# Attention in a two-layer trunk: row sums from a column of ones, the mask added on TensorE, head pairs on the two halves of the array

## The chip, the cores and the metric

The kernel runs on one core of one Trainium2 chip. The metric is the device time of one execution in microseconds (us); where several runs are given, it is their median. The engines are called by the profile's names: PE is the matrix engine (TensorE) and PEld its weight loads, DVE the vector engine, ACT the scalar engine, POOL the GpSimd engine, SP the queue that starts most transfers. PSUM is the small memory that PE writes to and that DVE and ACT read.

## The reference

Two layers. Each has a feed-forward block, a token mixer, a second feed-forward block and a norm. The mixer projects the normed rows (512 tokens, width 1024) once and splits the result into three groups of heads whose outputs are joined and projected back:

```python
y_conv = conv_module(u_conv, ...)                 # gated, causal depthwise conv of width 31, LayerNorm, swish: 384 channels
y_swa  = sliding_window_attention(q, k, v, sinks) # 6 query heads over 2 key/value heads of width 64
y_mem  = memory_attention(qm, mk, mv)             # 4 heads of width 64 over 256 memory tokens
h = h + concat([y_conv, y_swa, y_mem]) @ w_out
```

Both attentions are softmax attentions over at most 256 keys. In the sliding window each block of 128 queries sees its own block of keys and the one before, cut by a band:

```python
scores = einsum(q, keys of this block and the one before) * 64 ** -0.5
scores = where(0 <= rel < 128, scores, -inf)
probs = softmax(concat([scores, sink]))[..., :-1]   # the sink enters the sum, and has no value
out = einsum(probs, v)
```

All of it is fp32. The kernel holds its large projections as a high and a low part in a 32-bit format that PE multiplies in one pass (fp32r) and makes three products of them; the small attention products are plain fp32.

## The kernel before

A layer's feed-forward blocks are long runs of fp32r matmuls, and they are not changed, but for the memory's keys and values, which are made in the middle of the first block. The change is in the mixer. It is written as a list of steps (`ORDER`, line 45): three input projections of the convolution (`c`), queries and keys (`q`), values (`v`), four steps `r0` to `r3` for the memory attention and four steps `w0` to `w3` for the window, one for each block of 128 tokens, then the convolution's taps (`t`) and its norm and swish (`s`). That list is not the order on the chip. A scheduler of the language reorders the instructions of the whole program by its own estimate of times, and each engine then runs its instructions strictly in the resulting order: an instruction that waits holds up all behind it on its engine.

The steps of the attention, with the names that the text uses:

- **Scores.** For a pair of heads (a *pair* is the two heads that share 128 columns, one on partitions 0 to 63 and one on 64 to 127) one fp32 matmul multiplies the 128 rows of queries with a key tile of twice the width, in which each head's other half is zero (`kz` for the window, `mz` for the memory): lines 716 and 733. PSUM tiles `mm` take the result. The scores are negated, so that the row's maximum is a minimum.
- **Minimum.** In a window one DVE instruction per head (line 719) adds the band's mask, writes the masked scores back and gives the row's minimum, which starts from the sink. In the memory steps one reduction per pair does (line 734).
- **Exponential.** ACT (line 685), one instruction per head, which also sums its row into `den` by `accum_out`; that appears in the trace as a further ACT instruction that reads the accumulator.
- **Weighted sum** (`weighted`). PE transposes the 128x128 blocks of probabilities into a `pt` tile (line 690), ACT copies it to `aux` (line 692), PE multiplies it with the values into `po` (line 695).
- **Normalise and transpose** (`attended`). For a window DVE adds the sink's part to `den` (line 724) and inverts it (725); DVE multiplies `po` with the inverse (line 701), PE transposes the result into a `cf` tile (line 704), ACT and DVE split it into the high and the low part (lines 135 and 136).
- **Taps.** The depthwise convolution is 93 DVE instructions in a layer, 3 of line 741 and 90 of line 744, each on 128x512 elements. They depend on nothing in the attention. Their sum over channels goes through PE at line 753 to the norm and swish (lines 753 to 763).
- **Output projection.** PE first multiplies the attention's five tiles (120 matmuls for 8 output tiles), then the convolution's three (72 matmuls), all of 512 columns in fp32r.

## Time and profile before

| | us |
|---|---|
| median of 3 runs | 1847.12 |
| lowest and highest run | 1841.6, 1849.46 |
| the profiled execution's own time | 1840.85 |
| its span | 1839.1 |
| PE busy in the span | 1777.9 (97%) |
| DVE, ACT, POOL busy | 1297.8, 895.5, 188.3 |

The profiled execution is one of its own, 6.3 us below the median of the three. Its span leaves out 1.75 us around the program. In the rows of a timeline the first number is the start and the second the duration of one instruction, or of a few alike that follow each other; a duration of PE is longer than the step to the next start, since matmuls are pipelined, so times of PE are best taken from start to start. A plain fp32 matmul shows as two records, one for each of its two passes, and a transpose as one. The attention of layer 0 lies between 468 and 526 us and that of layer 1 between 1371 and 1429 us.

### The profile page before, as it was taken

The numbers are of one execution on the slowest core, as the hardware profiler recorded it, in microseconds if no ns is written. First come the engines' busy times: TensorE is split into PE (matmuls) and PEld (weight loads), VectorE is DVE, ScalarE is ACT, GpSimd is POOL, SyncE is SP. The second block draws the span as 40 slices with busy tenths as digits, with TensorE's granted clock in tenths as the row PEclk, the third lists the DMA queues.
The fourth block names the chain that finished last, engine by engine and source line by source line (L and its number), as shares of the span: only waits on it lengthen the run. The fifth ranks groups of instructions, "written<-read, shape, count | busy, mean of one in ns | idle before, by whom it ended". The sixth has DMA issues, their size and how long they took to land.

```text
span 1839.1 us, 28085 instructions
## 1 busy us (share of the span) xinstructions
PE 1777.9 (97%) x10892; PEld 1581.9 (86%) x10892; DVE 1297.8 (71%) x1978; ACT 895.5 (49%) x1459; POOL 188.3 (10%) x194
## 2 busy tenths in 40 slices
PE   6999999998899999999999999999989999999997
PEld 5989999877677989898888898988776889898986
DVE  7967666579956866666678586666789577675755
ACT  5556444354656535453565463535456455353532
POOL 4001000005101000000010010000240010000000
PEclk8999999999999999999999999999999999999998
DMA  9565645263038556565465565643530576474622
GB/s 278 125 172 159 177 130 155 63 159 101 15 77 200 118 141 167 143 169 141 133 154 139 160 170 141 170 118 92 117 105 1 144 162 158 134 181 122 171 78 75
DMA packets 92437, 248.87 MB, mean 135 GB/s; under 512 B 9488, under 2 KB 11792, under 8 KB 92304
## 3 DMA queue, kind: packets, MB, share of 16 engines
q1 hardware_dynamic: 76752, 190.45, 34.0%
q0 software_dynamic: 15552, 56.63, 17.3%
q8 instruction: 85, 1.39, 0.3%
q14 instruction: 48, 0.39, 0.1%
HBM read 244.95 MB, written 2.10 MB: 134 GB/s over the span
## 4 chain that ended last, share of the span: by engine, by line
PE 76%; DVE 10%; issue 7%; DMA 4%; ACT 2%; POOL 1%; SPq 0%; POOLq 0%; DVEq 0%; ACTq 0%
PE mm L162 11%; PE mm L163 10%; PE mm L161 10%; PE po L163 8%; PE po L161 8%; PE po L162 8%; PE pt L161 5%; PE pt L162 5%; PE pt L163 5%; DVE there L744 3%; DVE wlo L136 1%; DMA wlo<-in_w1a 1%; DVE xlo L146 1%; DMA wlo<-in_wconv 1%; DVE st L229 1%
## 5 line engine op out<-in xcount | busy, mean ns | idle before, releaser
L135 ACT ACTIVATE whi<-raw 128x1024 fp32r<-128x1024 f32 (+4 forms) x372 | 342.3, 924 | 513.3 <-PE mm L162 263.9
L136 DVE TENSOR_TENSOR wlo<-raw,whi 128x1024 fp32r<-128x1024 f32 (+4 forms) x372 | 392.0, 1056 | 123.8 <-ACT whi L135 122.5
L162 PE MATMUL mm<-glo,whi 128*128 128x512 f32 x752 | 293.9, 391 | 1.0 <-DVE glo L136 1.0
L161 PE MATMUL mm<-ghi,whi 128*128 128x512 f32 x752 | 289.8, 391 | 5.2 <-ACT ghi L379 4.5
L163 PE MATMUL mm<-ghi,wlo 128*128 128x512 f32 x752 | 292.8, 389 | 0.0
L163 PE MATMUL po<-mh,wlo 128*128 128x256 f32 x864 | 244.6, 283 | 1.4 <-DVE wlo L136 1.4
L161 PE MATMUL po<-mh,whi 128*128 128x256 f32 x864 | 244.8, 283 | 0.0
L162 PE MATMUL po<-ml,whi 128*128 128x256 f32 x864 | 244.6, 283 | 0.0
L161 PE MATMUL pt<-xhi,whi 128*128 128x256 f32 x864 | 243.4, 283 | 1.0 <-DVE g L347 0.7
L163 PE MATMUL pt<-xhi,wlo 128*128 128x256 f32 x864 | 243.9, 283 | 0.0
L162 PE MATMUL pt<-xlo,whi 128*128 128x256 f32 x864 | 243.8, 283 | 0.0
L443 DVE SCALAR_TENSOR_TENSOR h<-mm,h 128x512 f32<-128x512 f32 x128 | 87.7, 688 | 134.5 <-PE mm L163 134.5
L161 PEld LDWEIGHTS mm<-ghi,whi 128*128 128x128 f32 x752 | 140.9, 188 | 35.9 <-ACT ghi L379 6.2
L161 PEld LDWEIGHTS pt<-xhi,whi 128*128 128x128 f32 x864 | 165.1, 192 | 3.0 <-DVE g L347 1.1
L163 PEld LDWEIGHTS po<-mh,wlo 128*128 128x128 f32 x864 | 165.8, 192 | 1.6 <-DVE wlo L136 1.6
L162 PEld LDWEIGHTS mm<-glo,whi 128*128 128x128 f32 x752 | 141.4, 188 | 30.0 <-DVE glo L136 1.9
L162 PEld LDWEIGHTS pt<-xlo,whi 128*128 128x128 f32 x864 | 165.7, 192 | 1.1
L161 PEld LDWEIGHTS po<-mh,whi 128*128 128x128 f32 x864 | 165.8, 192 | 0.9 <-ACT part L366 0.2
L163 PEld LDWEIGHTS mm<-ghi,wlo 128*128 128x128 f32 x752 | 141.2, 188 | 29.2
L162 PEld LDWEIGHTS po<-ml,whi 128*128 128x128 f32 x864 | 165.8, 192 | 0.6
L163 PEld LDWEIGHTS pt<-xhi,wlo 128*128 128x128 f32 x864 | 165.5, 192 | 0.0
L744 DVE SCALAR_TENSOR_TENSOR there<-ypad,par,there 128x512 f32<-128x512 f32 x180 | 133.7, 759 | 0.7
(272 smaller groups left out, 3306.4 us busy)
## 6 DMA issues: line engine op xcount, KB each, us to landing
raw<-in_w2a SPq DMA_DIRECT2D x48, 384.0 KB, 3.7
raw<-in_w2b SPq DMA_DIRECT2D x48, 384.0 KB, 4.0
raw<-in_w1a SPq DMA_DIRECT2D x26, 512.0 KB, 3.7
raw<-in_w3a SPq DMA_DIRECT2D x26, 512.0 KB, 4.3
raw<-in_w1b SPq DMA_DIRECT2D x26, 512.0 KB, 3.8
raw<-in_w3b SPq DMA_DIRECT2D x26, 512.0 KB, 3.7
wsum<-in_w1a SPq DMA_DIRECT2D x18, 512.0 KB, 4.5
wsum<-in_w3a SPq DMA_DIRECT2D x18, 512.0 KB, 4.5
```

Source lines behind the costliest of these rows:

```text
L135: A.activation(hi, x, AF.Copy)
L136: on.tensor_tensor(out=lo, in0=x, in1=hi.bitcast(F32), op=ALU.subtract)
L146: V.scalar_tensor_tensor(out=lo, in0=x, scalar=col, in1=hi.bitcast(F32), op0=ALU.mult, op1=ALU.subtract)
L161: T.matmul(ps, a[0], b[0], start=first, stop=False, **more)
L162: T.matmul(ps, a[0], b[1], start=False, stop=False, **more)
L163: tail[0] = T.matmul(ps, a[1], b[0], start=False, stop=last, **more)
L229: V.tensor_tensor(out=self.sums[0], in0=self.sums[0], in1=sq, op=ALU.add)
L443: V.scalar_tensor_tensor(out=h[:, d, :], in0=ps, scalar=0.5, in1=h[:, d, :], op0=ALU.mult, op1=ALU.add)
L744: V.scalar_tensor_tensor(out=cv[:, c, :], in0=ypad[:, c, j : j + S], scalar=conv_w[:, c, j : j + 1], in1=cv[:, c, :], op0=ALU.mult, op1=AL ...
```

## The change

- **Key tiles without zeros.** `kT` and `mT` hold both heads, one on each half of the partitions. `scored` makes two matmuls per pair, each on 64 rows of the array: head 0 on rows 0 to 63 and head 1 on rows 64 to 127, of 256 columns each (128 in `w0`) where there was one of 512 (256 in `w0`). Head 0 of every pair goes to one PSUM tile and head 1 to another.
- **The mask on PE.** In a window each of these tiles is first written by an fp32r matmul of the identity with the mask (line 686), and the scores are added to it in PSUM.
- **Two pairs per minimum.** A window handles its pairs as (0, 1) and (2). One reduction takes the minimum of the same head of two pairs (line 736), and a small instruction then takes the sinks in (line 737). The memory steps take both pairs at once (line 752).
- **Sums from a column of ones.** The values get a 65th column of ones, so the weighted sum gives the sum of the row in column 64 of `po`. ACT's `accum_out` goes, and a window's `den` becomes `po`'s column 64 plus the sink's part (line 742), a memory step's inverse comes straight from it (line 755).
- **Fewer, wider splits.** Two neighbouring tiles of `y` are split at once, and the transposes of `attended` use a `pt` tile instead of `cf`. The copies that spread keys over two zero-padded tiles become one copy, and the zero fills become fills of the ones.

```diff
+        def scored(cs, W, q, k, masked):
+            pp = [mm().rearrange("p (c k) -> p c k", c=2)[:, 0 : len(cs), 0:W] for _ in range(2)]
+            if masked:
+                for ps in pp:
+                    T.matmul(ps, identr, maskr[:, 256 - W : 256].unsqueeze(1).to_broadcast([P, len(cs), W]), start=True, stop=False,
+                             skip_group_check=True)
+            for n, c in enumerate(cs):
+                for i in range(2):
+                    e = blk(i, HD)
+                    T.matmul(pp[i][:, n, :], q(c)[e], k(c)[e], start=not masked, stop=True, skip_group_check=True)
+            return pp
...
-                A.activation(pr[:, i, 0 : nk * P], scores[:, i, 0 : nk * P], AF.Exp, bias=nm[:, n : n + 1], scale=-1.0,
-                             accum_out=den[:, n : n + 1])
+                A.activation(pr[:, i, 0 : nk * P], scores[i], AF.Exp, bias=nm[:, n : n + 1], scale=-1.0)
...
-            V.tensor_tensor(out=heads(z), in0=po, in1=rd.unsqueeze(2).to_broadcast([P, n, HD]), op=ALU.mult)
-            pt = bank([P, c1 - c0, P], "cf")
+            V.tensor_tensor(out=heads(z), in0=po[:, :, 0:HD], in1=rd.unsqueeze(2).to_broadcast([P, n, HD]), op=ALU.mult)
+            pt = bank([P, c1 - c0, P], "pt")
...
-            po = bank([P, NH, HD], "po")
-            for c in range(CC):
-                ps = bank([P, 2, 256], "mm")
-                T.matmul(ps[:, :, 0:W], qT[:, c, blk(b)], kz[:, :, b0 * P : b0 * P + W], start=True, stop=True)
+            po = bank([P, NH, HD + 1], "po")
+            nmv, sinks = (x.rearrange("p (c i) -> p i c", i=2) for x in (nm, nsink[:, l, :]))
+            for cs in ((0, 1), (2,)):
+                pp = scored(cs, W, lambda c: qT[:, c, blk(b)], lambda c: kT[:, b0 * P : b0 * P + W], True)
+                z = slice(cs[0], cs[-1] + 1)
                 for i in range(2):
-                    n = 2 * c + i
-                    V.tensor_tensor_reduce(out=ps[:, i, 0:W], in0=ps[:, i, 0:W], in1=mask[:, 256 - W : 256], scale=1.0,
-                                           scalar=nsink[:, l, n : n + 1], op0=ALU.add, op1=ALU.min, accum_out=nm[:, n : n + 1])
-                weighted(c, nk, ps, nm, den, lambda j, i: vn[:, b0 + j, blk(i, HD)], po)
+                    V.tensor_reduce(out=nmv[:, i, z], in_=pp[i], axis=AX.X, op=ALU.min)
+                V.tensor_tensor(out=nmv[:, :, z], in0=nmv[:, :, z], in1=sinks[:, :, z], op=ALU.min)
+                for n, c in enumerate(cs):
+                    weighted(c, nk, [ps[:, n, :] for ps in pp], nm, lambda j, i: vn[:, b0 + j, i, :], po)
             V.tensor_tensor(out=es, in0=sink, in1=nm, op=ALU.add)
             A.activation(es, es, AF.Exp)
-            V.tensor_tensor(out=den, in0=den, in1=es, op=ALU.add)
-            V.reciprocal(rd, den)
+            V.tensor_tensor(out=rd, in0=po[:, :, HD], in1=es, op=ALU.add)
+            V.reciprocal(rd, rd)
             attended(b, 0, CC, po, rd)
```

The scheduler puts the new instructions in another order, and moves old ones too. Three places show it. The numbers behind the names tell buffers apart.

**Place 1: DVE in layer 0, ahead of the minima of window step `w1`.** Line 744 before and line 763 now are taps; a row that ends in x11 is eleven of them. Before (the tiles `mm_4533` and `mm_4549` hold the scores of `w1`):

```order
L722 TENSOR_TENSOR a1_4473<-rw_98,a0_4472 128x6
L744 SCALAR_TENSOR_TENSOR there_3738<-ypad_106,par_96,there_3738 128x512
L136 TENSOR_TENSOR glo_3755<-cf_4422,ghi_3754 128x128
L744 SCALAR_TENSOR_TENSOR there_3738<-ypad_106,par_96,there_3738 128x512
L724 TENSOR_TENSOR a2_4474<-a2_4474,a1_4473 128x6
L744 SCALAR_TENSOR_TENSOR there_3738<-ypad_106,par_96,there_3738 128x512
L136 TENSOR_TENSOR glo_3755<-cf_4422,ghi_3754 128x128
L725 RECIPROCAL a3_4475<-a2_4474 128x6
L719 ISA mm_4533,a0_4528<-mm_4533,cst_94,nsink_110 128x256
```

and now, where the tiles `mm_4529` and `cf_4530` hold the scores of the first two pairs of `w1`:

```order
L740 TENSOR_TENSOR a1_4465<-rw_98,a0_4464 128x6
L763 SCALAR_TENSOR_TENSOR there_3737<-ypad_106,par_96,there_3737 128x512 x2
L136 TENSOR_TENSOR glo_3753<-pt_4459,ghi_3752 128x2x128
L763 SCALAR_TENSOR_TENSOR there_3737<-ypad_106,par_96,there_3737 128x512 x11
L742 TENSOR_TENSOR a2_4466<-po_4467,a1_4465 128x6
L736 TENSOR_REDUCE a0_4525<-mm_4529 128x2
L736 TENSOR_REDUCE a0_4525<-cf_4530 128x2
L736 TENSOR_REDUCE a0_4525<-mm_4564 128x1
L736 TENSOR_REDUCE a0_4525<-mm_4565 128x1
```

From the first minimum of `r0` on, both orders hold the same 37 taps of layer 0 (36 in layer 1). Before, 13 of them (12 in layer 1) stand ahead of the first minimum of `w1`, and the others are spread up to the end of `r3`. Now 34 (32 in layer 1) stand ahead of it, and none behind the minima of `w2`.

**Place 2: PE in layer 0, from the first transposes of `w1` to the scores of `w2`.** Before:

```order
L690 MATMUL pt_4539<-cst_94,uu_3744 128x128 x4
L716 MATMUL mm_4601<-here_3737 128x512
L690 MATMUL pt_4555<-cst_94,pr_3747 128x128 x2
L704 MATMUL cf_4518<-cst_94,aux1_3742 128x128 x3
L716 MATMUL mm_4617<-here_3737 128x512
L716 MATMUL mm_4633<-here_3737 128x512
L695 MATMUL po_4532<-here_3737,aux0_3741 128x64 x4
```

and now, where `mm_4602` and `mm_4637` belong to head 0 of the pairs and `cf_4603` and `mm_4638` to head 1:

```order
L703 MATMUL pt_4542<-cst_94,uu_3742 128x128 x4
L686 MATMUL mm_4602<-maskr_117 128x512
L691 MATMUL mm_4602<-here_3736 128x256 x2
L686 MATMUL cf_4603<-maskr_117 128x512
L691 MATMUL cf_4603<-here_3736 128x256 x2
L686 MATMUL mm_4637<-maskr_117 128x256
L691 MATMUL mm_4637<-here_3736 128x256
L686 MATMUL mm_4638<-maskr_117 128x256
L691 MATMUL mm_4638<-here_3736 128x256
L708 MATMUL po_4528<-here_3736,aux0_3739 128x65 x4
```

In every window the products of one half of the array stand together, and a mask product on all 128 rows stands between the two halves. Only in the memory steps do the halves stand side by side, in 3 of the 8 steps alternating and in 5 as two of one half and then two of the other. Over a layer PE changes 39 times between products on 128 and on 64 rows.

**Place 3: DVE and PE in layer 0, from the end of `w1` to `w2`.** DVE now:

```order
L742 TENSOR_TENSOR a2_4527<-po_4528,a1_4526 128x6
L736 TENSOR_REDUCE a0_4598<-mm_4602 128x2
L736 TENSOR_REDUCE a0_4598<-cf_4603 128x2
L736 TENSOR_REDUCE a0_4598<-mm_4637 128x1
L743 RECIPROCAL a2_4527<-a2_4527 128x6
L736 TENSOR_REDUCE a0_4598<-mm_4638 128x1
L737 TENSOR_TENSOR a0_4598<-a0_4598,nsink_110 128x2x2
L714 TENSOR_TENSOR aux1_3740<-po_4528,a2_4527 128x384
```

and PE now:

```order
L708 MATMUL po_4528<-here_3736,aux0_3739 128x65 x8
L717 MATMUL pt_4590<-cst_94,aux1_3740 128x128 x3
L703 MATMUL pt_4615<-cst_94,uu_3742 128x128 x4
L691 MATMUL mm_4674<-mT_114,there_3737 128x256 x2
L691 MATMUL cf_4675<-mT_114,there_3737 128x256 x2
```

The first DVE row reads column 64 of `po_4528`, which the first PE row completes; before, the sum at its place (line 724) read nothing that PE makes. The minima of `w2` stand behind it on DVE, the multiplication of `w1` (line 714) behind those, and on PE the transposes of that product (line 717) stand straight behind the weighted sum.

66 lines of the change are left out of this document (35 added, 31 removed).

## The prediction

> **What bounds the kernel now.** I read the page first, then the stages of the two mixers by windows, then the timeline of DVE and PE in them.
>
> ```profile
> span 1839.1 us, 28085 instructions
> PE 1777.9 (97%) x10892; PEld 1581.9 (86%) x10892; DVE 1297.8 (71%) x1978; ACT 895.5 (49%) x1459; POOL 188.3 (10%) x194
> PE 76%; DVE 10%; issue 7%; DMA 4%; ACT 2%; POOL 1%; SPq 0%; POOLq 0%; DVEq 0%; ACTq 0%
> ```
>
> PE sets the time nearly everywhere; what the change is worth is decided where PE waits, in the attention.
>
> ```profile
> core 0: us, PE busy (x) PEld busy (x) DVE busy (x) ACT busy (x) POOL busy (x), PEclk, DMA share, GB/s
> 468.50:486.90 18.40, 16.43 (x92) 11.22 (x93) 18.34 (x49) 12.60 (x43) 3.29 (x3) 1.00 0.06 19
> 486.90:490.50 3.60, 0.71 (x7) 0.48 (x6) 3.60 (x16) 0.95 (x4) 0.95 (x1) 0.83 0.00 0
> 490.50:495.00 4.50, 4.50 (x14) 3.10 (x15) 4.43 (x12) 3.31 (x15) 0.00 (x0) 0.50 0.01 2
> 495.00:520.00 25.00, 24.75 (x164) 18.95 (x163) 23.69 (x67) 17.71 (x62) 0.00 (x0) 0.98 0.00 1
> 526.00:554.40 28.40, 28.40 (x139) 23.86 (x138) 9.51 (x17) 10.42 (x17) 2.52 (x4) 1.00 0.51 128
> ```
>
> In layer 0 DVE is full from 468.5 to 495 (26.4 of 26.5 us), for most of it with taps. It feeds PE too late once, at 486.9 to 490.5, and PE then runs at a granted clock of 0.50 for 4.5 us. From there on PE is full, and its output projection hides the swish, whose work on DVE and ACT is light. So the time of a mixer is when `w1`'s first transposes start on PE, plus what PE has left from there to the next stage.
>
> ```profile
> 490.45 1.14 PE L690 MATMUL pt<-cst,uu 128*128 128x128 f32 x4 [2.88 <-ACT uu L685]
> 491.38 1.91 PE L716 MATMUL mm<-here 128*128 128x512 f32 x2
> 503.94 1.02 PE L716 MATMUL mm<-here 128*128 128x512 f32 x2
> 504.80 0.49 PE L704 MATMUL cf<-cst,aux 128*128 128x128 f32 x3
> 505.13 1.90 PE L695 MATMUL po<-here,aux 128*128 128x64 f32 x16
> 506.86 0.61 PE L690 MATMUL pt<-cst,uu 128*128 128x128 f32 x4
> 507.31 1.02 PE L716 MATMUL mm<-here 128*128 128x512 f32 x2
> 570.75 0.39 PE L161 MATMUL mm<-xhi,whi 128*128 128x512 f32 x1
> 570.98 0.39 PE L162 MATMUL mm<-xlo,whi 128*128 128x512 f32 x1
> 1394.78 0.89 PE L690 MATMUL pt<-cst,uu 128*128 128x128 f32 x4 [2.05 <-ACT uu L685]
> 1473.75 0.39 PE L161 MATMUL mm<-xhi,whi 128*128 128x512 f32 x1
> ```
>
> The rows of 570.75 and 1473.75 begin the next stage, so that rest takes 80.3 us in layer 0 and 79.0 us in layer 1 now. From start to start: a score product of 512 columns takes 0.86 us (both passes), a weighted sum 2 x 1.73/16 = 0.216, a transpose 0.45/4 = 0.11, an fp32r product of 512 columns 0.227 (0.23 in the row).
>
> **What the change moves ahead of `w1`.** DVE costs, from start to start:
>
> ```profile
> 471.20 0.68 DVE L734 TENSOR_REDUCE m<-mm 128x2 f32<-128x512 f32 x1
> 471.80 0.41 DVE L514 TENSOR_REDUCE hs<-hsq 128x4 f32<-128x256 f32 x1
> 472.13 0.68 DVE L734 TENSOR_REDUCE m<-mm 128x2 f32<-128x512 f32 x1
> 472.73 0.41 DVE L519 TENSOR_TENSOR gg<-gg,rsq 128x256 f32<-128x256 f32 x1
> 473.06 0.74 DVE L744 SCALAR_TENSOR_TENSOR there<-ypad,par,there 128x512 f32<-128x512 f32 x1
> 473.72 0.54 DVE L741 TENSOR_SCALAR there<-ypad,par 128x512 f32<-128x512 f32 x1
> 474.18 0.16 DVE L515 TENSOR_SCALAR hv<-hs 128x4 f32<-128x4 f32 x1
> 486.94 0.45 DVE L719 CUSTOM_DVE_ANT_0 mm<-mm,cst,nsink 128x256 f32<-128x256 f32 x1
> 487.31 0.14 DVE L719 DVE_READ_ACCUMULATOR2_ANT a<- 128x1 f32 x1
> 507.96 0.55 DVE L701 TENSOR_TENSOR aux<-po,a 128x384 f32<-128x384 f32 x1
> 508.43 0.28 DVE L136 TENSOR_TENSOR glo<-cf,ghi 128x128 fp32r<-128x128 f32 x1
> 508.62 0.48 DVE L719 CUSTOM_DVE_ANT_0 mm<-mm,cst,nsink 128x256 f32<-128x256 f32 x1
> 1374.14 0.68 DVE L734 TENSOR_REDUCE m<-mm 128x2 f32<-128x512 f32 x1
> ```
>
> A tap takes 0.66, a reduction of 512 elements 0.60 and of 256 0.33, other work on 256 elements 0.33, line 701 0.47, a split of 128 elements 0.19, small ones 0.09. The taps never wait, so DVE runs its order without a gap, as it does now. Counted from the first minimum of `r0` (471.20 and 1374.14, unmoved, since the same 56 or 57 taps stand ahead of it), the new order holds, up to the multiplication of `w0` that PE's transposes of line 717 wait for ahead of `w1`: 36 taps (23.8), one line 760 (0.5), minima of `r0` and `r1` (2.4), of `w0` (about 1.1) and of `w1` (1.9), three line 714 (1.1), two splits (0.7), two scalings of queries (0.7) and a dozen small ones (1.1), 33.1 us in all. In layer 1 there are 34 taps and one scaling and a 0.6 us multiplication, 31.9. With 0.4 us for three transposes and the handover, `w1`'s first transposes start at 504.7 and 1406.4 instead of 490.45 and 1394.78: **+14.3 and +11.6 us**. DVE's work itself is less, not more: a window takes 2 x 0.60 + 2 x 0.33 + 0.2 = 2.1 where six times 0.40 were, and five splits become three, some 3 us a layer; but the gain lies behind `w1`, where DVE no longer sets the time.
>
> **What PE has left from there.** 65 transposes (7.2), 52 weighted sums (11.2; the 65th column costs nothing, since 64 columns in 0.108 a pass are far above what 512 in 0.43 make of them), 20 score products of 256 columns, each at half of 0.86 (8.6), masks of `w2` and `w3` (2 x (2 x 0.227 + 2 x 0.113) = 1.4), line 772 (0.9), 192 products of the output projection (43.5) and the swish's sums and broadcast (1.7 and 0.8, in the chain of waits): 75.2 us.
> ```profile
> 533.46 1.68 PE cf L186 x16
> 540.52 0.89 PE pt L199 x8
> ```
>
> The same count of the old work gives 73.8, so 6.5 and 5.2 us of the old 80.3 and 79.0 are waits and the slow clock. To the 75.2 I add what the new order makes of waits.
>
> *The sums from the ones.* Line 742 reads what the last weighted sum writes, the next step's minima wait behind it on DVE, the product for line 717 behind these, and PE has line 717 straight after the weighted sum. So PE stands still for line 742, the minima but the last, 743 and 714, and the handovers:
>
> ```profile
> 521.30 0.42 DVE L701 TENSOR_TENSOR aux<-po,m 128x256 f32<-128x256 f32 x1 [0.24 <-PE po L695]
> 489.83 0.47 ACT L685 ACTIVATE uu<-mm,a 128x256 f32<-128x256 f32 x1 [1.95 <-DVE a L719]
> ```
>
> DVE waited 0.24 us there for PE, ACT in the second row for DVE; I take 0.35 for both handovers of a wait. Between `w1` and `w2` that is 2.6 + 0.35, between `w2` and `r2` 1.85 + 0.35 less 0.55 of scores that fill it, between `r2` and `w3` 1.95 + 0.35, between `w3` and `r3` 1.85 + 0.35: 9.1 us. Exponentials and copies that nothing on PE covers (`r2`'s copies, `w3`'s last minimum and first exponentials at 0.47 each) add about 2. **11 us a layer.** ACT no longer reads accumulators, which shortens these a little and nothing else, since ACT is at 71% of its time there (17.71 of 25 us).
>
> *Array halves and changes of mode.* No two halves run side by side in a window: a mask product on all rows stands between. In `r2` and `r3` at best one product of 0.43 in a pair is hidden, 0.9 a layer at most; I take none. What a change between 128 and 64 rows costs, no row shows. Below nothing is excluded by the count above; the upper end is a pipeline that empties at each, which is what a product's duration exceeds its spacing by:
>
> ```profile
> L163 PE MATMUL mm<-ghi,wlo 128*128 128x512 f32 x752 | 292.8, 389 | 0.0
> L161 PEld LDWEIGHTS mm<-ghi,whi 128*128 128x128 f32 x752 | 140.9, 188 | 35.9 <-ACT ghi L379 6.2
> ```
>
> 0.389 less 0.227 is 0.16, and with a weight load laid bare 0.35. Of the 39 changes of a layer 20 come after `w1`'s first transposes: 0 to 7 us; I take half of 0.16 each, 1.6, as loads are mostly pulled ahead. [...]
>
> *The clock.* By the costs above PE has some 17 us of work in the 33 us ahead of `w1` (`r0`, `r1`, `w0`, the scores of `w1`), and eleven taps in a row (7.3 us) leave it a gap just before. After 3.6 us with little work it ran at 0.50 for 4.5 us; the same again costs 2.2.
>
> **The sum.** 75.2 + 11 + 1.6 + 2.2 = 90.0 for 80.3 and 79.0: +9.7 and +11.0. With +14.3 and +11.6 that is +46.6, from 1840.85 of the profiled execution to 1887. That execution lies 6.3 under the median, whose sum would be 1894. I say **1889**. What I cost at nothing: the mask's copy and the fills at the start lie under the first weight transfers, and would cost their length, under 1 us, without that cover; the fewer key copies on ACT lie under PE's projections.
>
> **The rivals.** *The delay alone*: PE finds other work in every wait, and the clock holds. The rest is then 75.2, and the sum +14.3 + 11.6 - 5.1 - 3.8 = +17, 1864. For it speaks that PE hardly waits after 495 now; against it that the order leaves nothing between the weighted sum and line 717.
>
> *Faster: the halves overlap.* Were head 0 and head 1 of each pair side by side, nine pairs of windows would save 0.43, three of `w0` 0.22 and eight of the memory 0.43, 8 us a layer, less 2.4 of masks: -11 in all, 1836, from the point at which PE and not DVE sets `w1`'s start. [...] The order keeps the halves apart in windows and the taps ahead of `w1`, so I give it little; that the change does not do what its title says about halves is the likelier reading.
>
> *No change*: DVE free of taps from `w2` on serves PE so fast that waits vanish, and the old slow clock goes too. That needs 8.5 us a layer less than the delay alone, more than all the waits there are now (6.5 and 5.2): 1841 to 1847 at the very best.
>
> *Changes of mode dear*: 0.35 each and the slow clock after every wait, 5 us: 75.2 + 11 + 7 + 7 = 100, sum +67, 1911; with longer handovers 1920.
>
> **How the numbers follow.** Forecast with its own spread 0.80; delay alone 0.09; dear changes 0.06; no change 0.03; overlap 0.02. A difference of under 0.5% (9 us) cannot be told from none here. So slower 0.95, same 0.03, faster 0.02. The range: below, the delay with half of the waits and no mode cost, 1840.85 + 17 + 11 = 1869, lowered a little for the delay alone, 1865; above, dear changes, 1915.
>
> **What would show it.** In the changed profile `w1`'s first transposes start near 504.7 and 1406.4, with a PE wait for DVE ahead of them and a clock near 0.5 after; PE waits at line 717, put down to line 714, some 2 us four times a layer; the next stage begins near 595 in layer 0; behind `w2` DVE is no longer full; starts of line 691 lie 0.43 apart. I am wrong if `w1` starts as early as now, if line 717 waits for nothing, or if the rest takes under 80 us.

## The result and the profile after

| | before | after |
|---|---|---|
| median, us | 1844.62 | 1947.58 |
| lowest and highest run | 1841.6, 1849.46 | 1946.65, 1951.77 |
| ratio (95% interval) | | 1.056 [1.0536, 1.0583] |
| profiled execution's span | 1839.1 | 1944.9 |
| mean granted clock | 0.988 | 0.946 |

The change makes the kernel 103 us slower; forecast were 42 to 47. The direction was right, the forecast size was less than half of the measured one, and the time lies above the range of 1865 to 1915. The page of the changed kernel (span; busy time, share and instructions of each engine):

```profile
span 1944.9 us, 28120 instructions
PE 1853.8 (95%) x11004; PEld 1641.7 (84%) x11004; DVE 1298.5 (67%) x1914; ACT 881.9 (45%) x1352; POOL 186.5 (10%) x191
```

PE is busy 76 us longer, but hardly with more work. The next two fences show the windows view, for each layer from the first score product of the memory to `w1`'s first transposes, and from there to the next stage's first product. First the changed kernel:

```profile
core 0: us, PE busy (x) PEld busy (x) DVE busy (x) ACT busy (x) POOL busy (x), PEclk, DMA share, GB/s
468.31:510.86 42.55, 30.39 (x127) 22.13 (x128) 38.44 (x75) 13.71 (x35) 4.55 (x3) 0.63 0.03 8
510.86:620.71 109.85, 98.89 (x436) 79.32 (x436) 39.02 (x81) 42.20 (x84) 5.00 (x5) 0.77 0.25 64
1423.69:1464.43 40.74, 30.10 (x127) 22.17 (x126) 37.38 (x71) 14.04 (x36) 2.27 (x2) 0.64 0.03 8
1464.43:1578.82 114.39, 103.39 (x436) 81.52 (x436) 39.64 (x82) 41.61 (x83) 5.00 (x5) 0.74 0.25 61
```

and the kernel before, in the same columns:

```profile
468.49:490.45 21.96, 17.11 (x97) 11.65 (x97) 21.90 (x63) 13.51 (x47) 4.24 (x3) 0.97 0.05 16
490.45:570.75 80.30, 79.04 (x411) 62.83 (x411) 55.55 (x126) 46.23 (x120) 4.99 (x5) 0.96 0.35 88
1371.75:1394.78 23.03, 17.81 (x97) 12.22 (x95) 21.09 (x58) 14.10 (x48) 2.28 (x2) 0.93 0.05 15
1394.78:1473.75 78.97, 76.58 (x410) 61.29 (x411) 55.49 (x127) 46.62 (x120) 4.99 (x5) 1.00 0.36 90
```

The columns give the length of the stretch, the busy time of each engine, and the granted clock (PEclk). Three quantities come out of each row: PE's idle time (length less busy), its work at full clock (busy times clock) and the loss to the clock (busy times one less the clock). PEclk is a mean over the whole length, idle time included, and has two digits, so the last two are good to some 3 us in a long stretch. In layer 0 and layer 1 together the work grows by 5 us (from 185.6 to 191.1), the idle time by 31 (from 13.7 to 44.7), and the loss to the clock by 67 (from 5.0 to 71.7). These three make the 103 us. Counted only where PE is busy, with the pieces of full and of half clock that the traces record, the work grows by 7 and the loss by 65: the reading stays.

In the timeline of PE in the changed kernel (start, duration, line, with the wait ahead and what ended it in brackets) stand the places that the prediction spoke of:

```profile
468.31 0.48 PE L691 MATMUL mm<-mT,there 64*128 64x256 f32 x1 [0.65 <-ACT there L551]
468.32 0.48 PE L691 MATMUL cf<-mT,there 64*128 64x256 f32 x1
...
510.20 0.88 PE L717 MATMUL pt<-cst,aux 128*128 128x128 f32 x3 [4.28 <-DVE a L740]
510.86 1.06 PE L703 MATMUL pt<-cst,uu 128*128 128x128 f32 x4
511.58 0.78 PE L686 MATMUL mm<-maskr 128*128 128x512 f32 x1
514.28 0.79 PE L686 MATMUL cf<-maskr 128*128 128x512 f32 x1
...
530.38 0.87 PE L717 MATMUL pt<-cst,aux 128*128 128x128 f32 x3 [2.81 <-DVE a L737]
...
554.48 0.69 PE L717 MATMUL pt<-cst,aux 128*128 128x128 f32 x2 [2.11 <-DVE aux L714]
...
567.66 0.87 PE L717 MATMUL pt<-cst,aux 128*128 128x128 f32 x3 [2.30 <-DVE aux L714]
...
1464.43 1.06 PE L703 MATMUL pt<-cst,uu 128*128 128x128 f32 x4
```

`w1`'s first transposes start at 510.86 and 1464.43. The waits at line 717 are there, 2 to 4 us each. The memory's products on the two halves run side by side (468.31 and 468.32). A window's do not, and at half clock a mask and two products take 2.7 us (511.58 to 514.28). The windows view shows the point that decides:

```profile
479.13:533.75 54.62, 42.57 (x138) 30.62 (x138) 31.91 (x69) 14.18 (x40) 2.99 (x2) 0.50 0.00 1
533.75:543.99 10.24, 8.20 (x48) 5.93 (x47) 2.01 (x5) 2.65 (x6) 0.00 (x0) 1.00 0.00 0
543.99:571.30 27.31, 21.93 (x88) 18.29 (x89) 6.58 (x19) 8.93 (x22) 0.00 (x0) 0.50 0.00 1
1465.00:1475.00 10.00, 10.00 (x24) 5.71 (x23) 0.76 (x3) 0.88 (x3) 1.27 (x1) 0.50 0.00 0
```

From 1465 to 1475 PE never waits, and its clock is 0.50 all the time. The first three rows are the pieces of half and full clock in layer 0. In all traces here the clock in an attention goes between 1.00 and 0.50 in pieces of 3.41 us or whole multiples of it: these three are 16, 3 and 8 such lengths, and the slow ones in the two attentions of the kernel before are 2 and 1.

### The profile page after: what moved, and what is told of

It reads as the page before. It is cut to its first block, busy times and chain, and to the rows that moved or that the text cites. A ratio compares the mean times of both kernels' runs of the same rounds, so it can differ in the third digit from the quotient of the medians.

```text
span 1944.9 us, 28120 instructions
## 1 busy us (share of the span) xinstructions
PE 1853.8 (95%) x11004; PEld 1641.7 (84%) x11004; DVE 1298.5 (67%) x1914; ACT 881.9 (45%) x1352; POOL 186.5 (10%) x191
## 4 chain that ended last, share of the span: by engine, by line
PE 79%; DVE 10%; issue 6%; DMA 2%; ACT 1%; POOL 1%; SPq 0%; DVEq 0%; POOLq 0%; ACTq 0%
PE mm L161 10%; PE mm L162 10%; PE mm L163 10%; PE po L163 8%; PE po L161 8%; PE po L162 8%; PE pt L162 5%; PE pt L161 5%; PE pt L163 5%; DVE there L763 3%; PE po L708 2%; PE mm L691 2%; PE pt L703 1%; DVE wlo L136 1%; DMA wlo<-in_w1a 1%
```

## Experiments

Line numbers in an experiment's rows are its own. The kernels with "u" undo parts of the change in the changed kernel; those with "a" make one part alone in the kernel before. The table reads the stretch from the memory's first score product to the next stage in layer 0 in the way shown above, with the same error. Each ratio is to runs of the kernel before that were made together with it, whose medians lie between 1842.4 and 1846.7, so times of kernels made at different times compare to some 4 us. The scheduler makes a new order for each kernel, and each price includes that.

| kernel | us | ratio to before (95%) | stretch, us | idle | loss to clock | work at full clock |
|---|---|---|---|---|---|---|
| before | 1844.6 | | 102.3 | 6.1 | 2.9 | 93.3 |
| after | 1947.6 | 1.056 [1.0536, 1.0583] | 152.4 | 23.1 | 34.9 | 94.4 |
| u_rows | 1913.3 | 1.0371 [1.0351, 1.0391] | 138.4 | 26.6 | 19.0 | 92.8 |
| u_ones | 1930.9 | 1.0466 [1.0422, 1.051] | 151.2 | 9.4 | 42.6 | 99.3 |
| u_mask | 1933.8 | 1.0485 [1.0468, 1.0501] | 151.9 | 20.8 | 39.3 | 91.8 |
| u_pair | 1980.9 | 1.0738 [1.0719, 1.0757] | 171.5 | 18.4 | 53.6 | 99.6 |
| u_rows_ones | 1879.2 | 1.0184 [1.0167, 1.0201] | 120.3 | 12.4 | 10.8 | 97.1 |
| u_mask_ones | 1918.4 | 1.0391 [1.0371, 1.0412] | 142.6 | 11.0 | 40.8 | 90.9 |
| u_rows_mask_ones | 1890.5 | 1.0241 [1.0224, 1.0259] | 131.5 | 15.7 | 20.8 | 95.0 |
| u_all4 | 1877.4 | 1.0167 [1.0144, 1.019] | 117.1 | 9.8 | 10.7 | 96.5 |
| u_allrows_ones | 1878.5 | 1.0179 [1.0161, 1.0197] | 123.1 | 12.7 | 13.2 | 97.1 |
| u_all5 | 1865.7 | 1.0118 [1.0101, 1.0134] | 115.3 | 15.6 | 3.0 | 96.7 |
| u_onebank | 1878.1 | 1.0188 [1.0169, 1.0208] | 121.6 | 16.4 | 10.5 | 94.7 |
| a_ones | 1896.2 | 1.0286 [1.0271, 1.03] | 127.0 | 19.6 | 12.9 | 94.5 |
| a_pt | 1883.5 | 1.02 [1.018, 1.022] | 120.5 | 16.1 | 10.4 | 94.0 |
| after_cf | 1965.4 | 1.0652 [1.0634, 1.0669] | 163.8 | 16.5 | 50.1 | 97.2 |
| a_mask | 1841.5 | 0.9988 [0.9976, 0.9999] | 98.6 | 3.7 | 0 | 95.0 |
| best | 1838.5 | 0.9978 [0.9966, 0.9991] | 97.3 | 3.3 | 0 | 94.0 |

The work at full clock stays between 91 and 100 us whatever is changed (between 92 and 101 when counted where PE is busy). All large differences are idle time and clock. One thing sorts the kernels. In the six whose windows keep the halves (after, `u_ones`, `u_mask`, `u_pair`, `u_mask_ones`, `after_cf`) the longest unbroken piece of half clock in this stretch is 55 to 119 us. In the others it is at most 20.5 us.

### One part undone in the changed kernel

`u_rows` pads the windows' keys to all rows again:

```diff
-        kT = here[:, 1536:2048]
+        kz = here[:, 1536:2560].rearrange("p (i s) -> p i s", i=2)
+        for i in range(2):
+            G.memset(kz[blk(1 - i, HD), i, :], 0.0)
...
-                    T.matmul(pp[i][:, n, :], q(c)[e], k(c)[e], start=not masked, stop=True, skip_group_check=True)
+                    T.matmul(pp[i][:, n, :], q(c) if masked else q(c)[e], k(c, i) if masked else k(c)[e], start=not masked, stop=True, skip_group_check=True)
```

> The windows' keys are padded with zeros to all 128 rows again, as before; all else (mask on TensorE, column of ones, two pairs a minimum, the memory's products on halves) stays as changed. In the changed kernel PE works from 1464.4 to 1482 us without a gap over 0.3 us and still runs at a granted clock of 0.50, where the kernel before, after its gap, was at full clock 4.5 us later. Theory A (products on 64 rows, one half at a time, count for too little to get the clock back): the granted clock is back within some 5 us after each wait, the rest of a mixer after w1's first transposes falls from 109.9 and 114.4 us to some 90, and the time falls by 40 to 50 us, to 1900. Theory B (the waits for DVE behind the column of ones keep the clock down, rows do not matter): only the changes of mode go, some 0.2 us each at full clock and 0.4 at half, about 25 a layer: 10 to 20 us less, 1930, and the clock stays near 0.5 in the attention.

`u_ones` takes the sums from the exponentials again:

```diff
+                             accum_out=den[:, n : n + 1])
...
-            V.tensor_tensor(out=rd, in0=po[:, :, HD], in1=es, op=ALU.add)
+            V.tensor_tensor(out=den, in0=den, in1=es, op=ALU.add)
```

> The sums come from the exponentials' accumulators again, without a column of ones; all else as changed. Line 742 then no longer reads what the last weighted sum writes. Theory A (rows): the waits ahead of the transposes of a step shorten from some 2.3 us to under 1.5, four or five a layer, but the clock stays at 0.50 through most of the attention: 10 to 20 us less in all, 1930. Theory B (waits): the clock stays up once the waits are short, and the time falls by 40 to 60 us, to 1895.

Measured: 34 and 17 us less than the changed kernel. In layer 0, first `u_rows`, then `u_ones` (windows view):

```profile
469.99:608.35 138.36, 111.78 (x562) 93.86 (x563) 77.53 (x156) 54.79 (x117) 9.54 (x8) 0.83 0.21 54
```

```profile
468.72:619.94 151.22, 141.86 (x563) 109.80 (x563) 78.92 (x156) 58.90 (x157) 9.54 (x8) 0.70 0.19 49
520.00:530.00 10.00, 10.00 (x29) 6.82 (x28) 1.85 (x5) 0.94 (x3) 0.00 (x0) 0.50 0.00 0
```

With full rows PE still waits as much as in the changed kernel (26.6 us idle), but the loss to the clock falls from 34.9 to 19.0. Without the column of ones the idle time falls from 23.1 to 9.4, and the loss to the clock grows: from 520 to 530 PE waits for nothing and runs at 0.50. The profiled execution of `u_ones` is the slowest of its four (1937.9; the lowest is 1922.6), but it is still faster than the changed kernel. Theory B, that the waits behind the column of ones hold the clock down, falls with that row. Theory A stands in part: the time of `u_rows` lies between the two theories, and full rows do not bring the whole clock back.

`u_mask` adds the mask on DVE as before, with one `tensor_tensor_reduce` for each head. `u_pair` takes one pair at a time in windows and memory steps:

```diff
-            for cs in ((0, 1), (2,)):
+            for cs in ((0,), (1,), (2,)):
```

> The mask is added on DVE again in one operation with the minimum, one for each head (six a window); no mask product on TensorE; halves, column of ones and two pairs' scores at a time stay. With no full-row product between them, head 0 and head 1 of a pair can run side by side, as the memory's do in the changed kernel (four products in 0.97 us where four took 1.72 before). Theory A: two halves at once count as a full array and the clock comes back: 40 to 50 us less, 1900. Theory B (waits): masks and half of the changes of mode go, 8 us a layer at half clock, DVE's minima grow by 0.3 a window: 15 us less, 1932.

> One pair a minimum, as before: scores, mask and minima of one pair at a time, all else as changed. Theory A and B: three more mask products and more changes of mode a window, DVE's minima of 256 in place of 512 elements at 0.33 in place of 0.30 a head: 0 to 10 us more, 1950 to 1960. A third theory (D, taking two pairs at once holds four banks and lengthens the chain from the first score to the last weighted sum): the waits ahead of line 717 shorten and the time falls by 15 us or more.

Measured: 14 less and 33 more. `u_mask` took the time of theory B and not of A (39.3 us lost to the clock). But it does not test A, since its order does not put the halves side by side either. In layer 0 none of the 48 passes of its windows' products runs at once with one of the other half, and in layer 1 four do. Timeline of `u_mask` (a tile holds scores of one half):

```profile
510.65 0.69 PE L703 MATMUL pt<-cst,uu 128*128 128x128 f32 x2
511.27 2.07 PE L691 MATMUL cf<-here 64*128 64x256 f32 x4
513.27 1.11 PE L703 MATMUL pt<-cst,pr 128*128 128x128 f32 x4
```

Four passes on one half stand alone between transposes. What halves side by side do to the clock is therefore read from the second stream below. `u_pair` cost more than either theory gave, again by the clock (53.6), and theory D, by which it was to be faster, fell too.

### What the clock answers to

Two kernels add a stream of work on PE alone behind the last output of the kernel before; in the second, DVE makes the waits. Each ran once.

```diff
+            def run(n, *rows):
+                bb = [mm() for _ in rows]
+                for _ in range(n):
+                    for e, b in zip(rows, bb):
+                        T.matmul(b[:, 0:256], q[e], k[e], start=True, stop=True)
...
+            run(24, lo)
+            run(24, full)
+            run(44, lo)
+            run(24, full)
+            run(44, lo, hi)
...
```

> The kernel before, and behind its last output a stream of products on PE alone, without a wait: 24 products of 256 columns on one half (64 rows), 24 on all rows, 44 on one half, 24 on all rows, 44 pairs on both halves side by side, 24 on all rows, 120 transposes, 24 on all rows, 90 products of 65 columns with their weight loads, 24 on all rows, 8 times the changed kernel's pattern (mask of 512 columns on all rows, two products of 256 on 64 rows, for each half), 24 on all rows. It measures the granted clock by kind of work. Theory A: the first 64-row stretch stays at 0.50 for its 20 us, the first full-row one is at full clock within 5 us, the second 64-row stretch falls back to 0.50 although PE never stops; the pattern too. Theory B: the clock is full from 4 us on and stays there, whatever the rows.

> The kernel before, and behind its last output stretches of PE work with a wait of PE for a chain of some 16 DVE operations (about 8 us) ahead of each, so that each starts at a granted clock of 0.50: 24 products of 256 columns on all rows; 40 pairs of products side by side on both halves; 140 transposes; 80 products of 65 columns with their loads; 8 times the changed kernel's pattern of mask and products on halves; behind each but the first, 24 products on all rows. Then 12 stretches of 24 products on all rows with waits ahead of 2, 3, 4, 5, 6 and 8 DVE operations, twice over. Theory A2 (as the first stream showed: a wait drops the clock, and only some kinds of work get it back): all rows are at full clock within 5 us; the changed kernel's pattern and one or both of transposes and 65-column products stay at 0.50 to their end; both halves at once, unclear, since the kernel with mask and sums undone stayed at 0.50. Of the waits, those of 2 and 3 operations (under 2 us) do not drop the clock, those of 6 and 8 do. Theory B2 (any work without a gap gets it back in 5 us): all are at full clock 5 us after their start.

The first stream, timeline and windows of PE. The view merges rows that write the same tile: the first row is 24 products on one half, 24 on all rows and 44 on one half, and the second row shown is 88 products on both halves with 24 on all rows behind them.

```profile
1839.62 53.08 PE L860 MATMUL mm<-h 64*128 64x256 f32 x184 [5.45 <-DVE h L849]
1903.19 29.82 PE L860 MATMUL mm<-h 64*128 64x256 f32 x224
1932.85 13.26 PE L866 MATMUL cf<-cst,h 128*128 128x128 f32 x120
1956.31 20.21 PE L868 MATMUL mm<-h 128*128 128x65 f32 x180
1988.15 0.50 PE L884 MATMUL mm<-mr 128*128 128x512 f32 x1
1988.58 1.13 PE L886 MATMUL mm<-h 64*128 64x256 f32 x4
1989.64 0.50 PE L884 MATMUL mm<-mr 128*128 128x512 f32 x1
```

```profile
1855.00:1860.00 5.00, 5.00 (x13) 3.71 (x12) 0.00 (x0) 0.00 (x0) 0.00 (x0) 0.50 0.00 0
1865.00:1870.00 5.00, 5.00 (x24) 4.37 (x23) 0.00 (x0) 0.00 (x0) 0.00 (x0) 0.95 0.00 0
1885.00:1890.00 5.00, 5.00 (x25) 4.34 (x24) 0.00 (x0) 0.00 (x0) 0.00 (x0) 1.00 0.00 0
```

The first stretch on one half (24 products, 20.8 us) stays at 0.50 to its end, though PE never stops; the full rows behind it, begun at 1860.4, are at full clock some 5 us later (0.95 in the mean from 1865 to 1870). The second stretch on one half starts at full clock and keeps it (1885 to 1890). So A was wrong in its second part: in this stream work on half of the rows did not win the clock back in 20.8 us, and did not lose it in 19.2 us. On both halves side by side a product of 256 columns takes 0.22 us (88 of them in 19.2), on one half 0.43, as on all rows. In the pattern the mask takes 0.43 in place of 0.227, and two products 1.06 in place of 0.86: each change between 128 and 64 rows took 0.20 us more in this stream. The change from all rows to one half at the start of the second stretch on one half, with no mask in it, took the same: there the two passes about it start 0.31 and 0.32 us before the next, where passes otherwise take 0.216.

In the second stream each kind of work starts after a wait of some 8 us, at 0.50:

```profile
1918.09 17.48 PE L874 MATMUL mm<-cst,pz 128*128 128x128 f32 x140 [7.72 <-DVE pz L861]
1953.64 34.37 PE L876 MATMUL cf<-pz 128*128 128x65 f32 x160 [7.72 <-DVE pz L861]
...
2051.62 12.44 PE L868 MATMUL mm<-pz 128*128 128x256 f32 x48
2090.50 10.60 PE L868 MATMUL mm<-pz 128*128 128x256 f32 x48 [2.19 <-DVE pz L861]
2103.75 13.65 PE L868 MATMUL mm<-pz 128*128 128x256 f32 x48 [2.65 <-DVE pz L861]
2120.51 12.12 PE L868 MATMUL mm<-pz 128*128 128x256 f32 x48 [3.11 <-DVE pz L861]
...
2188.57 12.22 PE L868 MATMUL cf<-pz 128*128 128x256 f32 x48 [2.65 <-DVE pz L861]
2203.89 10.60 PE L868 MATMUL mm<-pz 128*128 128x256 f32 x48 [3.11 <-DVE pz L861]
```

```profile
1885.00:1890.00 5.00, 5.00 (x50) 4.41 (x48) 0.00 (x0) 0.00 (x0) 0.00 (x0) 1.00 0.00 0
1925.00:1930.00 5.00, 5.00 (x48) 5.00 (x47) 0.00 (x0) 0.00 (x0) 0.00 (x0) 1.00 0.01 3
1980.00:1985.00 5.00, 5.00 (x25) 5.00 (x25) 0.00 (x0) 0.00 (x0) 0.00 (x0) 0.50 0.00 0
2045.00:2050.00 5.00, 5.00 (x10) 2.55 (x10) 0.00 (x0) 0.00 (x0) 0.00 (x0) 0.50 0.00 0
```

Both halves side by side, begun at 1880, are at full clock by 1885. Transposes are so after some 4 us (140 in 17.48 where 15.5 would do at the first stream's 13.26 for 120; 1.00 from 1925 to 1930). Products of 65 columns, each with its own weight load, stay at 0.50 for all their 34 us. The changed kernel's pattern stays at 0.50 for all its 43.6 us. The last rows are 24 products on all rows behind waits of growing length: 10.60 us is full clock, more means that it was lost. Full rows of 256 columns needed 3 to 6 us to get it back (1.5 to 3.05 us over the 10.60, at half speed twice that). The six waits of 1.26 to 2.19 us did not lose it (10.60 each), 2.65 did both times, 3.11 once in two, and 4.0 both times (12.29 and 12.28). For these streams A2 holds, with the 65-column products and the pattern as the two kinds that stay down. The length of a wait is not the whole condition: 3.11 went either way, and in `u_ones` the clock fell near 480 us behind several waits of at most 1.4 us.

The share of the array that the work fills sorts the pieces in these traces. Take the pieces of 3.41 us around the two attentions in all 20 traces, and behind the kernel in the two streams. For each piece work out what share of the array's time its products fill. Each pass counts with its columns at the spacing of an unbroken run (0.216 us for 256 columns in fp32 and in transposes, 0.227 for 512 in fp32r, twice that at half clock), times its rows over 128; the sum is divided by 3.41.

| piece at | share | pieces | next piece at full clock |
|---|---|---|---|
| full clock | under 0.35 | 80 | none |
| full clock | 0.35 to 0.40 | 24 | mixed, the change near 0.38 |
| full clock | over 0.40 | 1309 | all |
| half clock | under 0.70 | 396 | none |
| half clock | 0.70 to 0.85 | 47 | mixed, the change near 0.78 |
| half clock | over 0.85 | 92 | 91 |

So in these 1948 pieces the clock fell behind those with a share under some 0.38 and came back behind those over some 0.78, and between the two it stayed as it was, but for single pieces near the two bounds. The three kinds of work that neither lost it nor won it back in the streams lie between: one half 0.50; a 65-column pass at half clock 0.110 us (65/256 of 0.432) of its 0.215, 0.51; the pattern at half clock, with a mask of 0.454 us on all rows and four passes of 0.432 on half of them, 1.32 of its 2.73, 0.48. That PE is busy did not decide: at half clock no bound on a piece's busy time does better than the guess that the clock never comes back, which is wrong for 108 of the 535 pieces; the bound of 0.78 on the share is wrong for 7. In the changed kernel the piece that ends at 479.13 has a share of 0.32, and of the sixteen behind it only the last, with 0.90, is over 0.70. In `u_ones` the piece that ends at 479.51 has 0.21. The two bounds are fitted to these traces, and no run was made to test them.

### Several parts undone

> Both the windows' full rows and the accumulators' sums are back; mask on TensorE and two pairs a minimum stay. With the sums alone undone, PE had hardly a wait left (each under 1 us) and still ran at 0.50 from 480 to 570 us; with the rows alone undone, its waits stayed (up to 4.5 us) and the clock came back in part (0.66 to 0.84). Theory A (the kind of work sets the clock, rows first): with both, the clock stays near full after w1 and the time is within 10 to 25 us of the kernel before, 1855 to 1870, less than the sum of the two single gains (34 and 17 us) would make it, 1897. If the gains only add (theory B, waits and changes of mode each by themselves): 1897.

> The halves and two pairs at a time stay; mask on DVE and sums by accumulators are back, so no mask product and no wait for a column of ones. Theory A: the clock is still at 0.50 through the attention, since all score products are on 64 rows, and the time stays far above the kernel before: 1915. If mask products or waits had kept the clock down: 1860.

> Full rows in the windows, mask on DVE and sums by accumulators: what is left of the change is two pairs' scores at a time, the memory's products on halves, and splits of two blocks at once. Theory A: the clock is at full nearly throughout, 1840 to 1860. If it stays above 1890, rows, mask and sums together do not explain the loss, and the order that comes of taking two pairs at a time does.

> Full rows in the windows, mask on DVE, sums by accumulators and one pair at a time: left of the change are the memory's products on halves, one product for each head where there was one for two, splits of two blocks at once and another bank for the last transposes. With two pairs at a time instead it took 1890.5. If taking two pairs at a time costs (scores, minima and exponentials of two pairs ahead of the first weighted sum): 1850 to 1860. If the halves of the memory's products cost, through the clock: near 1890.

> As the kernel with full rows in the windows and accumulators' sums (1879), but the memory's products on all rows too; mask on TensorE and two pairs a minimum stay. No product is on 64 rows any more. Theory A2: the clock is now full wherever PE has no wait of some 2 us, 0.99 in the mean, and the time 1850 to 1862. If it stays at 1879, the memory's halves cost nothing and transposes and weighted sums alone leave the clock at 0.50 after a wait.

Measured: 1879, 1918, 1890, 1877 and 1879. Rows and sums together give 68 us where the single gains add up to 51: in layer 0 both the idle time (12.4) and the loss to the clock (10.8) are short. That is nearer to theory A than to B, but 9 us above A's range. `u_mask_ones` came out as theory A said, though 12 of the 48 passes of its windows' products in a layer do run side by side. With rows, mask and sums undone it was to be 1840 to 1860 by theory A, and was 1890. `u_all4` came out between its two theories. `u_allrows_ones` took the second of its readings: without any product on 64 rows 13.2 us of layer 0 are still lost to the clock, so the halves are not needed for a loss. A weighted sum of 64 columns has the same share as one of 65: in the kernel before its pass takes 0.108 us, of which 64 columns fill 0.054 (64/256 of 0.216), 0.50. Something that all of these keep holds 30 us. Whether the mask is on PE or on DVE is worth 11 us in favour of PE there. The memory's halves are not the cause there, since `u_allrows_ones` has none and is no faster than `u_rows_ones`.

### What is left: the bank of the last transposes

> As the kernel with rows, mask, sums and pairs undone (1877), and the memory's products on all rows too. Left of the change: each head's scores in a bank of its own (two banks a pair out of four, where one of three held both heads before), splits of two blocks at once, another bank for the last transposes. In all kernels that keep two banks a pair, w1's first transposes start between 502 and 514 us, where the kernel before has 490.5. Theory K (banks: only two pairs are in flight, so w1's scores and minima come later and taps are scheduled ahead of them): w1's first transposes stay at 500 or later and the time stays above 1860. Theory M (the memory's halves hold the clock down at the start of the attention, 0.50 from 474 to 490 in the kernel with four undone): the time falls to 1845 to 1852 and w1's transposes to 492.

> As u_all5, but both heads of a pair in one bank again, by one product. Left of the change: splits of two blocks at once and another bank for the last transposes. Theory K: w1's first transposes are back at 490 to 493 and the time at 1840 to 1848. Theory M: no difference to u_all5.

> The kernel before with one word changed: the transposes of a finished step (line 704) go into one of the two banks that the exponentials' transposes use, as in the changed kernel, in place of a bank of their own. Theory P (these transposes stand in the queue of banks between the pairs: a pair of the next step gets no bank before the step's multiplication, transposes and splits are through): w1's first transposes start some 10 us later, at 500 or more, waits ahead of line 704 appear as in the kernel with one bank a pair (1878), and the time is 1865 to 1880. If the bank is innocent: 1840 to 1848, and what keeps u_onebank at 1878 stays open.

```diff
-            pt = bank([P, c1 - c0, P], "cf")
+            pt = bank([P, c1 - c0, P], "pt")
```

Theory K (two banks a pair) fell: one bank for both heads was slower (1878) than two (1866). Theory M, which gave no difference there, fell on that too, and this difference stays unexplained. For the memory's rows M held in part: with them on all rows the loss to the clock went from 10.7 to 3.0 and the time down by 9 us by the ratios (12 by the times), but not to the time before. The word in the diff above, alone in the kernel before, costs 39 us, 3.5 us more than the top of what theory P gave. Its timeline:

```profile
493.64 0.44 PE L704 MATMUL pt<-cst,aux 128*128 128x128 f32 x2 [1.98 <-DVE aux L701]
502.68 0.60 PE L690 MATMUL pt<-cst,uu 128*128 128x128 f32 x4
```

`w1`'s first transposes start at 502.68 in place of 490.45, and a wait of 1.98 us stands ahead of line 704, where the kernel before had none in this place. What is shown is that the bank does it; that the scheduler, bound to take turns between these transposes and those of the exponentials in two banks, then puts the next step's pairs later, is argued from the order. `u_onebank` keeps only this bank and the wider splits, and its ratio (1.0188) is that of the bank alone (1.0200): the bank is enough for the 30 us that were left.

> The changed kernel with the last transposes in a bank of their own, and the scores of two heads turning over three banks instead of four. Theory P: the waits ahead of line 717 shorten, since other pairs go on behind them, and the time falls by 15 to 40 us, to 1910 to 1930, though the granted clock stays low for the halves. If the column of ones alone makes these waits: no change, or slower for the bank that the scores lose (1945 to 1960).

It was 18 us slower, not faster, which is the second reading and 4 us more. The run changes two things at once, the bank of the last transposes and the banks of the scores, and cannot part what the one gains from what the other loses.

### One part alone in the kernel before

> The kernel before with the column of ones alone: the sums come from the 65th column of the weighted sums; mask on DVE, full rows, one pair a minimum. It prices the wait that line 742 makes: my prediction had 9.1 us of it a layer after w1. Theory A2 (a wait that drops the clock costs twice, but full-row products get it back in 3 to 5 us): 15 to 30 us more, 1860 to 1875. If other work fills the wait: 1845 to 1850.

```profile
492.52 0.69 PE L707 MATMUL cf<-cst,aux 128*128 128x128 f32 x2 [3.72 <-DVE aux L704]
503.60 0.80 PE L693 MATMUL pt<-cst,uu 128*128 128x128 f32 x4 [3.16 <-ACT uu L689]
```

It costs 54 us, nearly twice the top of what was expected: waits of 3 us ahead of `w1` and others through the attention, 19.6 us idle in layer 0, and 12.9 lost to the clock. The column of ones and the bank each make `w1` late by themselves: it starts 33.7 and 33.3 us behind the memory's first score product, where that is 22.0 in the kernel before. No run puts these two alone together, so what they cost in company is open; in the changed kernel, taking the column of ones out gains 17 us where it costs 54 alone.

> The kernel before with the mask on TensorE alone: one fp32r product of identity and mask ahead of each pair's scores in the windows, on all rows, then one minimum for both heads and a small one with the sinks, in place of two operations; nothing else of the change. PE has 12 products of 256 or 512 columns more a layer (about 2.5 us), DVE some 2 us a window less at most. Expected: 1842 to 1852, the same as before. If DVE's time ahead of w1 counts, up to 5 us less.

> The kernel before with the mask on TensorE (0.9988 of its time) and splits of two blocks at once, which take two instructions of DVE and ACT for four. Expected 1836 to 1843: DVE's 0.2 us a split lies behind w1, where little waits for it.

```diff
+                T.matmul(ps[:, :, 0:W], mr[:, 0:P], mr[:, P + 256 - W : P + 256].unsqueeze(1).to_broadcast([P, 2, W]), start=True, stop=False)
...
-                    V.tensor_tensor_reduce(out=ps[:, i, 0:W], in0=ps[:, i, 0:W], in1=mask[:, 256 - W : 256], scale=1.0,
-                                           scalar=nsink[:, l, n : n + 1], op0=ALU.add, op1=ALU.min, accum_out=nm[:, n : n + 1])
+                V.tensor_reduce(out=nm[:, 2 * c : 2 * c + 2], in_=ps[:, :, 0:W], axis=AX.X, op=ALU.min)
```

The mask on TensorE by itself, on all rows and with both heads in one bank, is 0.9988 of the time before (1841.5 us, just under the range given). With splits of two blocks at once, and the last transposes in their own bank, it is 0.9978 [0.9966, 0.9991], some 4 us less, as expected. That is under the half per cent that I had called no difference, but the interval leaves out 1. The intervals of the two kernels overlap, so what the splits add is not shown. Layer 0 of `best`:

```profile
473.05:570.39 97.34, 94.00 (x519) 74.98 (x519) 74.92 (x156) 59.17 (x158) 9.23 (x8) 1.00 0.29 76
```

The clock is 1.00 throughout and PE idles 3.3 us. This is the version that beats both kernels, by little.

## Why the prediction was wrong, step by step

**Direction: right; the causes named are there, but not the largest.** Slower was forecast, for a late `w1` and serial waits behind the column of ones, and both are in the trace. `a_ones` shows that the column of ones by itself makes such waits. But of the 103 us some 65 are loss to the clock, for which the sum had 2.2 us a layer.

**What PE has left from `w1`: right.** Work and changes of mode were summed to 76.8 us (75.2 + 1.6). The rows behind `w1` give 98.89 x 0.77 = 76.1 and 103.39 x 0.74 = 76.5 (77.9 and 77.6 when counted where PE is busy).

**Waits: right in size, in part by luck.** 11 us a layer were forecast. PE is idle for 11.0 in both layers (109.85 less 98.89, 114.39 less 103.39). In layer 0 the four waits at line 717 make 8.0 of it (2.81, 2.11, 2.30 and one of 0.74) where 9.1 were forecast, and the others 3.0 where 2 were.

**Changes of mode: mis-sized, small.** I took 0.08 each, by the row at most 0.16 with loads pulled ahead; the first stream shows 0.20 (a mask of 0.43 in place of 0.227), more than the whole 0.16 of which I took half. Over 20 changes that is 4.0 in place of 1.6.

**The clock: the step that failed.** "After 3.6 us with little work it ran at 0.50 for 4.5 us; the same again costs 2.2." Measured behind `w1`: 22.7 and 26.9 us by the rows above (21.0 and 25.8 when counted where PE is busy). The error was to price one episode (which cost some 3 by its own row, 79.04 x 0.04) and to take recovery for granted. In the kernel before, what followed the wait were transposes and 512-column products on all rows, and the clock was 0.98 in the mean from 495 to 520 (in the second stream transposes won it back in some 4 us, full rows in 3 to 6); in the changed kernel what follows are masks with products on half of the rows, and 65-column products, which stayed at 0.50 for 43.6 and 34 us in that stream. That the kind of work counts, by the share of the array that it fills, is read from `u_rows` (34.9 us lost in layer 0 became 19.0), the streams and the table of pieces. This term misses 42 to 45 us of the 57 that the sum is short. The rival "changes of mode dear" did put the slow clock after every wait, and gave it 5 us a layer on top of the 2.2.

**The delay of `w1`: right in kind, mis-sized and half explained.** +14.3 and +11.6 were forecast. From the memory's first scores to `w1` it takes 42.55 and 40.74 us in place of 21.96 and 23.03: +20.6 and +17.7. These 6 us each are the other 12 of the 57. The sum took DVE as never waiting and a tap as 0.66 us, and neither held. DVE in layer 0:

```profile
494.69 8.62 DVE L763 SCALAR_TENSOR_TENSOR there<-ypad,par,there 128x512 f32<-128x512 f32 x11
506.03 0.17 DVE L742 TENSOR_TENSOR a<-po,a 128x6 f32<-128x6 f32 x1 [2.72 <-PE po L708]
```

PE was already at half clock (0.63 and 0.64 in the mean of these stretches) and made DVE wait 2.7 us for its weighted sum; a split makes it wait another 0.7. In the run of eleven, and in one of six ahead of it, taps follow each other 0.79 us apart instead of 0.66, 2 us in all; why, no run shows. The rest is half a microsecond by which `r0`'s minimum comes later, and as much for the three transposes at half clock. (The terms of the 33.1 us add up to 33.3.) What in the change puts the taps ahead of `w1` the prediction did not ask: `a_pt` and `a_ones` show that the bank and the column of ones each make `w1` late. The bank was told in the change and had no price in the prediction.

**Halves side by side: as said in the windows,** with masks between. In the memory steps they do overlap (starts at 468.31 and 468.32), and little is left of it: in layer 0 the first transposes behind them start at 472.73 in place of 473.05.

What stays open: whether the two bounds on the share hold in a run made to test them, why one bank for both heads is slower than two (`u_onebank`), and why `u_pair` is so much slower with masks and halves (+33 us) and its counterpart without them faster (1890 to 1877).

## What to carry to other kernels

When an edit leaves PE idle for 2 to 3 us at a time, ask what PE does next. Here the price was not the wait alone: in layer 0 of the changed kernel the clock then stayed at 0.50 for 54.6 us, up to the first piece of 3.41 us with a share over 0.78 (0.90). In the second stream full rows, transposes and both halves at once were back at full clock within 3 to 6 us; 65-column products and the pattern of masks and halves were not in 34 and 43.6 us. Work out busy time times clock first: where it does not change, count neither products nor modes, but idle time and clock. And a tile moved to another bank is an edit of its own: one word in the kernel before cost 39 us.

## What the runs showed of the hardware

What won the granted clock back in the streams was not the same as what kept it. Work on half of the rows ran at 0.50 for 20.8 us from a slow start and at 1.00 for 19.2 us from a full one. 65-column products stayed at 0.50 for 34 us in the second stream, and at full clock in the first (180 passes in 20.21 us from 1956.31). Full rows had the full clock after 3 to 6 us and transposes after some 4; the 34 us of 65-column products and the 43.6 us of masks and halves, both without a gap, did not. So it was not being busy that counted in these traces, but the share of the array that the work fills: the clock came back behind pieces of 3.41 us with a share over some 0.78, and fell behind those under some 0.38, in the table above. Waits of 2.65 us were enough to lose it twice out of two, and one of 3.11 was not once out of two.
